# A hybrid decoder layer: gate buffers, load lead times and the minimum of a merge

## The chip, the cores and the metric

The kernel runs on one core of a Trainium2 chip. Its engines are TensorE (PE in the profile, PEld for its weight loads), VectorE (DVE), ScalarE (ACT), GpSimd (POOL) and SyncE (SP), which in this kernel issues the DMA transfers. The metric is the device time of one execution in microseconds.

## The reference

One layer on 2048 tokens of width 1024, in float32, batch 1:

```python
h = rms_norm(x, norm_w)
proj = h @ w_in                                  # 1024 -> all parts below
dn_qkv, dn_z, dn_b, dn_a, swa_q, swa_k, swa_v, swa_z, gates = split(proj)
# branch A: short causal convolution, then the gated delta rule in chunks of 64 (with a triangular solve)
o_dn  = rms_norm(gated_delta_rule(...), dn_norm_w) * silu(dn_z)
y_dn  = o_dn @ w_branch_dn                       # 512 -> 1024
# branch B: three groups of dilated window attention, merged by softmax over their log denominators
alpha = softmax(lses, axis=groups)
o_swa = sum(alpha * outs) * silu(swa_z)
y_swa = o_swa @ w_branch_swa                     # 512 -> 1024
merged = sigmoid(g_dn) * y_dn + sigmoid(g_swa) * y_swa
out = x + merged @ w_out                         # 1024 -> 1024
```

## The kernel before

A matrix product in float32 is made here of three products of rounded parts: each operand is split into a high part (ACT rounds it, L90) and a rest (DVE or POOL subtracts, L91), and TensorE adds high x high, high x rest and rest x high. Names ending in h and l are such pairs.

The program is written as one stream of TensorE work. Every few matmuls it calls `hook`, which counts a tick; `at(delay, fn)` puts other work that many ticks ahead into the stream. A tick in the last stage is half a block (12 matmuls). This fixes the order in which the program is written; the framework's scheduler then makes each engine's own order from it by its model of times and dependences. Through the attention TensorE, ACT, DVE and POOL are pinned to the written order, through the inversion ACT and POOL; in the last stage no engine is, SP neither. Each engine, SP included, then works through its order strictly one by one: an instruction that waits for a semaphore holds all behind it.

The stages: the input projection with the attention of branch B; z and g blocks of the projection (L723 to L725, whose results go to the scratch arrays zscr and gscr; an ACT step at L1158 reads each product), with the triangular inversion, the merge of the three attention groups and the scan of branch A in their background; and the last stage, which the change is mostly about.

*The merge* (`combine`, L1241 to L1279): for each of 16 tiles of 128 tokens it loads the three groups' outputs (oc, two buffers), takes the minimum over the groups on DVE (L1253, written to cs), and goes on with small POOL and ACT steps (`share`, `weigh`, `add`). The next tile's merge is 15 ticks later. DVE meanwhile works at the inversion (Z and M, L1023 to L1026).

*The last stage* (`run`, L1552 on) works on 8 groups of 256 tokens (nb). In each, `fin_y` makes 8 blocks (m) of 128 output columns of both branches: 24 matmuls of 128x256 (L1334 to L1336), the DVE multiply of the product by the gate (L1338, in place in the gate's tile gt4), the POOL sum of both branches (L1340) and the store of the sum to the scratch array mscr (L1341). The gate of a block is loaded from gscr by `g_load` (L1322) into one of four gt4 buffers, written two blocks ahead. A buffer is free again when its block's store has landed. There are 64 blocks, counted 0 to 63.

Beside it run: `o_plan`, which for the next group loads the branches' outputs (od, osw; L1286) and the z gates (two buffers, L1296), and prepares four operands by TensorE transposes (L1303), the DVE product with z (L1304), ACT (L1307) and POOL (L1308); and `wo_chunk`, which takes a quarter of the output weights raw from HBM (L1193), forms sums and splits, and parks two of them (T1 and T4) in scratch (L1202) through one pair of tiles th and tl. `fetch` (L1230) brings the parked ones back in the last group, four transfers of 1 MB.

Last come 8 `group`s of the output projection (L1411) by a seven-product scheme over two by two blocks; `m_load` (L1346) loads a group's merged values from mscr as one tile mt, and `m_op` forms and splits their sums (S1 to S4, L1367 on).

Of the kernel before, what the change touches and what calls it, by code (L numbers as in the profile page):

```python
# [17 lines left out]
H = 4  # L18
# [29 lines left out]
class Net:  # L48
# [1114 lines left out]
    def fin_setup(self, op, fp):  # L1163
        nc, i = self.nc, self.i
        self.fp = fp
        self.dnw = fp.tile([P, 1], F32, name="dnw", bufs=1)
        nc.sync.dma_start(self.dnw, dr(i["dn_norm_w"], 0, [[1, P], [1, 1]]))
        nc.vector.tensor_scalar(out=self.dnw, in0=self.dnw, scalar1=0.25, scalar2=None, op0=ALU.mult)
        self.oh0, self.ol0 = (op.tile([P, KT, 256], F32R, name=n, bufs=1) for n in ("oh", "ol2"))
        self.wbh, self.wbl = (a[:, 0:2].rearrange("p n k c -> p (n k c)").rearrange("p (m k c) -> p m k c", k=KT, c=P)  # L1170
                              for a in (self.hh, self.hl))
        self.W = {n: tuple(a[:, s, 4 * h:4 * h + 4, :] for a in (self.hh, self.hl))
                  for n, (s, h) in (("B11", (2, 0)), ("B21", (2, 1)), ("T3", (3, 0)), ("B22", (3, 1)),
                                    ("T1", (0, 0)), ("T4", (0, 1)))}
# [11 lines left out]
    def wo_chunk(self, c):  # L1186
# [34 lines left out]
        def fifth():  # L1221
            sub(r["B21"], r["B21"], r["T2"])
            put("T2", r["T2"], V)
        for d, fn in ((6, first), (8, second), (10, lambda: park("T1", r["B11"], V)), (12, fourth), (14, fifth),
                      (16, lambda: park("T4", r["B21"], nc.gpsimd))):
            self.at(d, fn)
# [5 lines left out]
    def comb_setup(self, cb):  # L1232
# [3 lines left out]
        self.comb_load(0)  # L1236
        self.at(8, lambda: self.combine(0))

    def comb_load(self, t):
        oc = self.oc = self.cb.tile([P, G, H, 130], F32, name="oc", bufs=2)  # L1240
        self.nc.sync.dma_start(oc.rearrange("p g h c -> p (g h c)"),  # L1241
                               dr(self.oscr, t * P * G * H * 130, [[G * H * 130, P], [1, G * H * 130]]))

    def combine(self, t):
        nc, cb, V = self.nc, self.cb, self.nc.gpsimd
        oc = self.oc
        if t < 15:
            self.comb_load(t + 1)
        sm = cb.tile([P, 4, 12], F32, name="cs", bufs=2)
        nm, ls = oc[:, :, :, 128], oc[:, :, :, 129]  # L1250
        mn, e, c, r = sm[:, 0, 0:4], sm[:, 1, :].rearrange("p (g h) -> p g h", h=H), \
            sm[:, 2, :].rearrange("p (g h) -> p g h", h=H), sm[:, 3, 0:4]
        nc.vector.tensor_reduce(out=mn.unsqueeze(2), in_=nm.rearrange("p g h -> p h g"), axis=mybir.AxisListType.X, op=ALU.min)  # L1253
        V.tensor_tensor(out=e, in0=mn.unsqueeze(1).to_broadcast([P, G, H]), in1=nm, op=ALU.subtract)
# [13 lines left out]
        def add(g):  # L1268
            o = oc[:, 0, :, 0:P]
            V.tensor_tensor(out=o, in0=o, in1=oc[:, g, :, 0:P], op=ALU.add)  # L1270
            if g == 2:
                nc.sync.dma_start(dr(self.osd, t * P * 512, [[512, P], [P, H], [1, P]]), o)
        self.at(1, share)
        for g in range(G):
            self.at(3 + g, lambda g=g: weigh(g))
        for g in (1, 2):
            self.at(4 + g, lambda g=g: add(g))
        if t < 15:
            self.at(15, lambda: self.combine(t + 1))  # L1279

    def o_load(self, t):
        nc, fp = self.nc, self.fp
        self.o = getattr(self, "o", {})
        od, os = (fp.tile([P, H, P], F32, name=n, bufs=2) for n in ("od", "osw"))
        for a, src in ((od, self.odn), (os, self.osd)):
# [8 lines left out]
    def z_load(self, t, b):  # L1294
        z = self.z[t, b] = self.fp.tile([P, H, P], F32, name="z", bufs=2)
        self.nc.sync.dma_start(z, dr(self.zscr, b * 4 * P * T + t * P, [[T, P], [P * T, 4], [1, P]]))  # L1296
# [13 lines left out]
    def o_plan(self, nb, d):  # L1310
        self.z = getattr(self, "z", {})
        for j, (t, b) in enumerate(((2 * nb, 0), (2 * nb, 1), (2 * nb + 1, 0), (2 * nb + 1, 1))):
            self.at(max(1, d + 3 * j - 4), lambda t=t, b=b: self.z_load(t, b))
            self.at(d + 3 * j, lambda t=t, b=b: self.o_prep(t, b))
# [3 lines left out]
    def g_load(self, i):  # L1318
        if i < 64:
            nb, m = divmod(i, 8)  # L1320
            gt = self.gt[i] = self.fp.tile([P, 2, 256], F32, name="gt4", bufs=4)
            self.nc.sync.dma_start(gt, dr(self.gscr, m * P * T + nb * 256, [[T, P], [8 * P * T, 2], [1, 256]]))  # L1322

    def fin_y(self, nb, m):
        nc = self.nc
        self.g_load(8 * nb + m + 2)
        gt = self.gt.pop(8 * nb + m)
# [15 lines left out]
    def m_load(self, g):  # L1343
        if g < 8:
            mt = self.mt[g] = (self.lp if g % 2 == 0 else self.p2).tile([P, KT, 256], F32, name="mt", bufs=1)
            self.nc.sync.dma_start(mt, dr(self.mscr, g * P * 2048, [[2048, P], [256, 8], [1, 256]]))  # L1346

# [8 lines left out]
    def m_op(self, q):  # L1356
# [4 lines left out]
        mt = self.mt[g]  # L1361
        part = {f"A{t + 1}{k + 1}": mt[:, 4 * k:4 * k + 4, t * P:(t + 1) * P] for t in range(2) for k in range(2)}
        name = PROD[i][0]
# [71 lines left out]
    def run(self):  # L1435
# [118 lines left out]
        self.gt, self.mt, self.ss = {}, {}, {}  # L1554
        self.g_load(0)
        self.g_load(1)
        for nb in range(8):
            if nb < 7:
                self.o_plan(nb + 1, 4)
            if nb in (0, 2, 4, 5):  # L1560
                self.wo_chunk((0, 2, 4, 5).index(nb))
            if nb == 6:
                self.at(8, lambda: self.m_load(0))
            for m in range(8):
# [3 lines left out]
                if nb == 7 and m < 4:  # L1568
                    self.at(3, lambda m=m: self.m_op(m))
        self.flush()  # L1570
# [49 lines left out]
```

## Time and profile before

| | us |
|---|---|
| median of 3 runs | 2406.46 (2401.22 to 2412.41) |
| the profiled execution | 2413.96 |
| its span | 2412.2 |
| TensorE busy in the span | 2298.8 |
| last stage, 1990 to 2250: TensorE busy | 218.6 of 260 |

The profiled execution ran at a granted clock of 0.983. A row of the windows gives the stretch, its length, the busy time of PE, PEld, DVE, ACT and POOL with their instructions, the granted clock, the DMA engines' busy share and GB/s. A row of waits reads "engine line <- what ended the wait: total, times, longest". A row of the timeline gives start, length, engine, line, operation and tiles, and in brackets the idle time before it and what ended that. SPq rows are the issuing of transfers, not the transfers themselves. A row of a group gives count, busy time and mean ns of one, then the idle time before it.

### The profile page before, as it was taken

How to read it: one execution, taken by the hardware profiler on the slowest of the kernel's cores; microseconds unless marked ns; L12 is line 12 of the kernel's file. 1: busy time of each engine (PE TensorE's matmuls, PEld its weight loads, DVE VectorE, ACT ScalarE, POOL GpSimd, SP SyncE). 2: the span in 40 equal slices, each digit the busy share in tenths (PEclk: the TensorE clock that was granted, in tenths of full speed). 3: DMA queues.
4: the chain of work that ended last, by engine and by line, in shares of the span. 5: the costliest groups of instructions: out<-in, count | busy, mean ns of one | idle time of the engine just before them, and what ended most of it. 6: DMA issues, size and time to landing. Idle time of an engine off the chain costs nothing. (4 is left out here: it accounts for less than half of the span.)

```text
span 2412.2 us, 43902 instructions
## 1 busy us (share of the span) xinstructions
PE 2298.8 (95%) x15120; PEld 2083.1 (86%) x15120; DVE 1353.8 (56%) x2786; ACT 978.5 (41%) x3151; POOL 1035.3 (43%) x1460
## 2 busy tenths in 40 slices
PE   7999999989999999999999999998999998888899
PEld 7999999889999999787788888886888888888687
DVE  6566576684445545537777759995244115323553
ACT  5345556643434445436666633334333232101121
POOL 6374275564213213206466634446332215433443
PEclk9999999999999999999999999999999999999999
DMA  9989989858887889744444443435767536855742
GB/s 303 322 285 317 276 262 288 258 174 273 249 243 245 259 251 297 207 121 127 129 126 120 110 133 118 134 111 186 201 193 214 168 122 199 226 166 146 240 167 92
DMA packets 556118, 485.82 MB, mean 201 GB/s; under 512 B 68152, under 2 KB 516984, under 8 KB 551928
## 3 DMA queue, kind: packets, MB, share of 16 engines
q1 hardware_dynamic: 555608, 482.95, 65.6%
q8 instruction: 120, 1.97, 0.3%
q14 instruction: 102, 0.84, 0.1%
q10 hardware_dynamic: 288, 0.07, 0.0%
HBM read 280.23 MB, written 202.67 MB: 200 GB/s over the span
## 5 line engine op out<-in xcount | busy, mean ns | idle before, releaser
L723 PE MATMUL mm<-hh,w 128*128 128x512 f32 x1152 | 465.3, 404 | 10.1 <-ACT gt L1158 10.1
L725 PE MATMUL mm<-hh,w 128*128 128x512 f32 x1152 | 459.2, 399 | 0.0
L724 PE MATMUL mm<-hl,w 128*128 128x512 f32 x1152 | 458.8, 398 | 0.0
L436 PE MATMUL mm<-w,hh 128*128 128x256 f32 x1760 | 326.8, 285 | 0.0
L723 PEld LDWEIGHTS mm<-hh,w 128*128 128x128 f32 x1152 | 221.2, 192 | 57.7 <-ACT gt L1158 11.4
L436 PEld LDWEIGHTS mm<-w,hh 128*128 128x128 f32 x1760 | 269.9, 189 | 0.0
L725 PEld LDWEIGHTS mm<-hh,w 128*128 128x128 f32 x1152 | 218.2, 189 | 47.4
L436 PE MATMUL mm<-hh 128*128 128x256 f32 x880 | 256.8, 292 | 0.0
L724 PEld LDWEIGHTS mm<-hl,w 128*128 128x128 f32 x1152 | 218.4, 190 | 42.6
L436 PE MATMUL mm<-hl,hh 128*128 128x256 f32 x880 | 249.0, 283 | 0.3 <-POOL hl L298 0.3
L436 PE MATMUL mm<-hh,hl 128*128 128x256 f32 x880 | 248.9, 283 | 0.0
L436 PE MATMUL mm<-w,hl 128*128 128x256 f32 x880 | 247.6, 281 | 0.0
L91 POOL TENSOR_TENSOR w<-raw,w 128x512 fp32r<-128x512 f32 x68 | 96.9, 1429 | 240.8 <-ACT w L90 223.5
L610 DVE CUSTOM_DVE_ANT_0 p<-sc,mask 128x128 f32<-128x128 f32 (+1 forms) x192 | 70.0, 365 | 216.1 <-PE sc L607 78.5
L371 POOL TENSOR_SCALAR st<-st 128x4 f32<-128x4 f32 x96 | 20.4, 212 | 372.4 <-ACT junk L370 370.4
L436 PEld LDWEIGHTS mm<-hl,hh 128*128 128x128 f32 x880 | 168.6, 192 | 0.8 <-POOL hl L298 0.8
L436 PEld LDWEIGHTS mm<-hh 128*128 128x128 f32 x880 | 168.6, 192 | 0.0
L436 PEld LDWEIGHTS mm<-hh,hl 128*128 128x128 f32 x880 | 168.2, 191 | 0.0
L436 PEld LDWEIGHTS mm<-w,hl 128*128 128x128 f32 x880 | 165.3, 188 | 0.0
L837 DVE SCALAR_TENSOR_TENSOR acc<-xr,cw,acc 128x512 f32<-128x512 f32 x144 | 121.1, 841 | 17.1 <-ACT acc L835 11.5
L594 ACT ACTIVATE kq<-tp 128x256 fp32r<-128x256 f32 x148 | 56.3, 381 | 178.9 <-PE tp L587 177.9
L613 ACT ACTIVATE p<-p,ol 128x128 f32<-128x128 f32 (+1 forms) x192 | 88.1, 459 | 64.0 <-DVE ol L610 63.7
(347 smaller groups left out, 5877.8 us busy)
## 6 DMA issues: line engine op xcount, KB each, us to landing
wdr<-w SPq DMA_DIRECT2D x56, 512.0 KB, 4.7
w<-wdr SPq DMA_DIRECT2D x54, 512.0 KB, 5.2
qk<-qks SPq DMA_DIRECT2D x212, 128.0 KB, 4.3
qks<-rec SPq DMA_DIRECT2D x96, 256.0 KB, 2.8
raw<-in_w_in_dram SPq DMA_DIRECT2D x68, 256.0 KB, 3.5
gscr<-gt SPq DMA_DIRECT2D x64, 256.0 KB, 3.4
gt<-gscr SPq DMA_DIRECT2D x64, 256.0 KB, 4.4
wdr<-hh SPq DMA_DIRECT2D x28, 512.0 KB, 4.6
```

The source lines that it names most:

```text
L91: eng.tensor_tensor(out=l, in0=raw, in1=h.bitcast(F32), op=ALU.subtract)
L371: nc.gpsimd.tensor_scalar(out=st[:, 0:4], in0=st[:, 0:4], scalar1=1.0 / P, scalar2=EPS, op0=ALU.mult, op1=ALU.add)
L436: mm = lambda x, y, **kw: nc.tensor.matmul(o, x, y, skip_group_check=True, **kw)
L594: nc.scalar.activation(h, src, AF.Copy)
L610: nc.vector.tensor_tensor_reduce(out=p[:, lo:hi], in0=sc[:, lo:hi], in1=self.mask[:, slot * P + lo:slot * P + hi], scalar=3e38, scale=-SCA ...
L613: self.at(1, lambda: nc.scalar.activation(p[:, lo:hi], p[:, lo:hi], AF.Exp, bias=ol[:, 128:129], scale=-1.0, accum_out=ol[:, 129:130]))
L723: nc.tensor.matmul(pr, wh[:, k, :], a, start=(k == 0), stop=False)
L724: nc.tensor.matmul(pr, wh[:, k, :], b, start=False, stop=False)
L725: nc.tensor.matmul(pr, wl[:, k, :], a, start=False, stop=(k == KT - 1))
L837: nc.vector.scalar_tensor_tensor(out=acc, in0=xr[:, j:j + 512], scalar=w[:, j:j + 1], in1=acc, op0=ALU.mult, op1=ALU.add)
```

## The change

- Gate tiles gt4: seven buffers instead of four; four loads are written before the first block, and each `fin_y` writes the load four blocks ahead instead of two.
- z tiles: three buffers instead of two, loads written eight ticks ahead of their use instead of four.
- The four `wo_chunk`s are given out from group 0 on at ticks 1, 29, 57 and 85 (in groups 0, 1, 3 and 5) instead of at the starts of groups 0, 2, 4 and 5, and their steps are one to three ticks later behind the raw loads.
- od and osw become halves of one tile "o" in the pool op, two buffers; the same buffers later hold the merged values of the even groups, in two half tiles with a load each. The odd groups use two half tiles in p2. The first merged group's load is written at the start of group 7 instead of eight ticks into group 6, its `m_op`s one tick later.
- The merge's minimum becomes a function of its own (`comb_min`), written six ticks ahead of its `combine`; the first combine is at tick 11 instead of 8, and share, weigh and add are one to two ticks later.

```diff
@@ wo_chunk
-        for d, fn in ((6, first), (8, second), (10, lambda: park("T1", r["B11"], V)), (12, fourth), (14, fifth),
-                      (16, lambda: park("T4", r["B21"], nc.gpsimd))):
+        for d, fn in ((9, first), (10, second), (11, lambda: park("T1", r["B11"], V)), (13, fourth), (15, fifth),
+                      (17, lambda: park("T4", r["B21"], nc.gpsimd))):
@@ comb_setup, comb_min, combine
-        self.at(8, lambda: self.combine(0))
+        self.at(6, self.comb_min)
+        self.at(11, lambda: self.combine(0))
+    def comb_min(self):
+        self.cs = self.cb.tile([P, 4, 12], F32, name="cs", bufs=2)
+        self.nc.vector.tensor_reduce(out=self.cs[:, 0, 0:4].unsqueeze(2), in_=self.oc[:, :, :, 128].rearrange("p g h -> p h g"),
+                                     axis=mybir.AxisListType.X, op=ALU.min)
-        nc.vector.tensor_reduce(out=mn.unsqueeze(2), in_=nm.rearrange("p g h -> p h g"), axis=mybir.AxisListType.X, op=ALU.min)
-        self.at(1, share)
+        self.at(2, share)
-            self.at(3 + g, lambda g=g: weigh(g))
+            self.at(5 + g, lambda g=g: weigh(g))
-            self.at(4 + g, lambda g=g: add(g))
+            self.at(6 + g, lambda g=g: add(g))
+            self.at(9, self.comb_min)
@@ o_load, z_load, o_plan
-        od, os = (fp.tile([P, H, P], F32, name=n, bufs=2) for n in ("od", "osw"))
+        o = self.op.tile([P, 4, 256], F32, name="o", bufs=2).rearrange("p a c -> p (a c)")
+        od, os = (o[:, x * 512:(x + 1) * 512].rearrange("p (h c) -> p h c", c=P) for x in range(2))
-        z = self.z[t, b] = self.fp.tile([P, H, P], F32, name="z", bufs=2)
+        z = self.z[t, b] = self.fp.tile([P, H, P], F32, name="z", bufs=3)
-            self.at(max(1, d + 3 * j - 4), lambda t=t, b=b: self.z_load(t, b))
+            self.at(max(1, d + 3 * j - 8), lambda t=t, b=b: self.z_load(t, b))
@@ g_load, fin_y
-            gt = self.gt[i] = self.fp.tile([P, 2, 256], F32, name="gt4", bufs=4)
+            gt = self.gt[i] = self.fp.tile([P, 2, 256], F32, name="gt4", bufs=7)
-        self.g_load(8 * nb + m + 2)
+        self.g_load(8 * nb + m + 4)
@@ m_load
-            mt = self.mt[g] = (self.lp if g % 2 == 0 else self.p2).tile([P, KT, 256], F32, name="mt", bufs=1)
-            self.nc.sync.dma_start(mt, dr(self.mscr, g * P * 2048, [[2048, P], [256, 8], [1, 256]]))
+            pool, name = (self.p2, "mt") if g % 2 else (self.op, "o")
+            mt = self.mt[g] = [pool.tile([P, 4, 256], F32, name=name, bufs=2) for _ in range(2)]
+            for x, a in enumerate(mt):
+                self.nc.sync.dma_start(a, dr(self.mscr, g * P * 2048 + x * 1024, [[2048, P], [256, 4], [1, 256]]))
@@ run
-        self.g_load(0)
-        self.g_load(1)
+        for j in range(4):
+            self.g_load(j)
-            if nb in (0, 2, 4, 5):
-                self.wo_chunk((0, 2, 4, 5).index(nb))
-            if nb == 6:
-                self.at(8, lambda: self.m_load(0))
+            if nb == 0:
+                for c in range(4):
+                    self.at(1 + 28 * c, lambda c=c: self.wo_chunk(c))
+            if nb == 7:
+                self.m_load(0)
-                    self.at(3, lambda m=m: self.m_op(m))
+                    self.at(4, lambda m=m: self.m_op(m))
```

*SP in the middle of the last stage.* Number behind a tile's name: which tile it is; a gate's tile has one number from its load to its store. Before, a load takes the buffer of the gate four blocks back: gt4_25267 that of gt4_25098, gt4_25299 that of gt4_25144.

```order
L1341 DMA mscr_217<-gt4_25098 128x256
L1322 DMA gt4_25267<-gscr_77 128x2x256
L1341 DMA mscr_217<-gt4_25144 128x256
L1322 DMA gt4_25299<-gscr_77 128x2x256
L1341 DMA mscr_217<-gt4_25178 128x256
L1286 DMA od_25410<-odn_75 128x512
L1341 DMA mscr_217<-gt4_25223 128x256
L1322 DMA gt4_25339<-gscr_77 128x2x256
L1296 DMA z_25366<-zscr_76 128x4x128
L1322 DMA gt4_25375<-gscr_77 128x2x256
L1341 DMA mscr_217<-gt4_25267 128x256
L1286 DMA osw_25411<-osd_216 128x512
```

Now it takes that of the gate seven blocks back: gt4_25285 that of gt4_25024, gt4_25323 that of gt4_25060, gt4_25363 that of gt4_25104, gt4_25404 that of gt4_25148.

```order
L1329 DMA gt4_25249<-gscr_77 128x2x256
L1303 DMA z_25280<-zscr_76 128x4x128
L1348 DMA mscr_217<-gt4_25024 128x256
L1348 DMA mscr_217<-gt4_25060 128x256
L1329 DMA gt4_25285<-gscr_77 128x2x256
L1329 DMA gt4_25323<-gscr_77 128x2x256
L1348 DMA mscr_217<-gt4_25104 128x256
L1329 DMA gt4_25363<-gscr_77 128x2x256
L1348 DMA mscr_217<-gt4_25148 128x256
L1303 DMA z_25338<-zscr_76 128x4x128
L1329 DMA gt4_25404<-gscr_77 128x2x256
L1348 DMA mscr_217<-gt4_25178 128x256
```

Each load still stands one to three rows behind the store of the tile whose buffer it takes; two stores, and then two loads, now sometimes stand together.

*SP at the end of the last stage.* hh_61 and hl_62 are the fetched weights, mt and o_25851 halves or wholes of group 0's merged values, o_26185 a half of group 2's. Before, from gate load 59 to gate load 62 (the load of group 0 as one tile stands far ahead):

```order
L1322 DMA gt4_25894<-gscr_77 128x2x256
L1341 DMA mscr_217<-gt4_25796 128x256
L1230 DMA hh_61<-wpkT10_218 128x2048
L1341 DMA mscr_217<-gt4_25834 128x256
L1230 DMA hl_62<-wpkT11_219 128x2048
L1322 DMA gt4_25926<-gscr_77 128x2x256
L1341 DMA mscr_217<-gt4_25864 128x256
L1322 DMA gt4_25962<-gscr_77 128x2x256
L1341 DMA mscr_217<-gt4_25894 128x256
L1230 DMA hh_61<-wpkT40_220 128x2048
L1230 DMA hl_62<-wpkT41_221 128x2048
L1322 DMA gt4_25996<-gscr_77 128x2x256
```

Now, from the second half of group 0's merged values on; gate load 59 stands two rows ahead, gate loads 60, 61 and 62 are in it, and the next row is gate load 63:

```order
L1355 DMA o_25851<-mscr_217 128x1024
L1329 DMA gt4_25854<-gscr_77 128x2x256
L1348 DMA mscr_217<-gt4_25638 128x256
L1329 DMA gt4_25884<-gscr_77 128x2x256
L1348 DMA mscr_217<-gt4_25676 128x256
L1355 DMA o_26185<-mscr_217 128x1024
L1348 DMA mscr_217<-gt4_25714 128x256
L1329 DMA gt4_25916<-gscr_77 128x2x256
L1231 DMA hh_61<-wpkT10_218 128x2048
L1348 DMA mscr_217<-gt4_25752 128x256
L1231 DMA hl_62<-wpkT11_219 128x2048
L1348 DMA mscr_217<-gt4_25782 128x256
```

Gate loads 60 to 62 stand ahead of the first fetch now, with stores between them, and two half loads of merged values stand among them. On DVE the additions that read group 0's halves now stand between the multiplies of blocks 54 (gt4_25638) and 55 (gt4_25676):

```order
L1345 SCALAR_TENSOR_TENSOR gt4_25638<-gt4_25638,mm_25784 128x512
L91 TENSOR_TENSOR ol2_22980<-o_25850,oh_22979 128x512
L1376 TENSOR_TENSOR raw_25945<-o_25850,o_25851 128x512
L1376 TENSOR_TENSOR raw_25947<-raw_25945,o_25850 128x512
L1345 SCALAR_TENSOR_TENSOR gt4_25676<-gt4_25676,mm_25822 128x512
```

so that the multiply of block 55 comes behind an addition that reads the second half.

*DVE in the inversion.* One piece of the difference, with a minimum of the merge (cs<-oc) among the steps of the inversion:

```order
 L1025 MEMSET M 128x1
 L1023 TENSOR_TENSOR Z<-M 128x3025
-L1253 TENSOR_REDUCE cs<-oc 128x4
 L1024 MEMSET M 128x64
 L1026 TENSOR_REDUCE M<-Z 128x55
 L1025 MEMSET M 128x1
 L1023 TENSOR_TENSOR Z<-M 128x3136
+L1248 TENSOR_REDUCE cs<-oc 128x4
 L1024 MEMSET M 128x64
 L1026 TENSOR_REDUCE M<-Z 128x56
```

The minimum moved behind the next round of the inversion here.

More of the change, by code (lines that the diff above doesn't have):

```diff
@@ L1165, in fin_setup @@
         self.fp = fp
+        self.op = op
         self.dnw = fp.tile([P, 1], F32, name="dnw", bufs=1)
@@ L1242, in comb_load @@
                                dr(self.oscr, t * P * G * H * 130, [[G * H * 130, P], [1, G * H * 130]]))
+    def comb_min(self):
+        self.cs = self.cb.tile([P, 4, 12], F32, name="cs", bufs=2)
+        self.nc.vector.tensor_reduce(out=self.cs[:, 0, 0:4].unsqueeze(2), in_=self.oc[:, :, :, 128].rearrange("p g h -> p h g"),
+                                     axis=mybir.AxisListType.X, op=ALU.min)
     def combine(self, t):
         nc, cb, V = self.nc, self.cb, self.nc.gpsimd
-        oc = self.oc
+        oc, sm = self.oc, self.cs
         if t < 15:
             self.comb_load(t + 1)
-        sm = cb.tile([P, 4, 12], F32, name="cs", bufs=2)
         nm, ls = oc[:, :, :, 128], oc[:, :, :, 129]
@@ L1361, in m_op @@
         mt = self.mt[g]
-        part = {f"A{t + 1}{k + 1}": mt[:, 4 * k:4 * k + 4, t * P:(t + 1) * P] for t in range(2) for k in range(2)}
+        part = {f"A{t + 1}{k + 1}": mt[k][:, :, t * P:(t + 1) * P] for t in range(2) for k in range(2)}
         name = PROD[i][0]
```

## The prediction

> **What bounds the kernel now.** I read the page first, then the last stage by windows, then the waits of SP's queue there, then that queue row by row.
>
> ```profile
> span 2412.2 us, 43902 instructions
> PE 2298.8 (95%) x15120; PEld 2083.1 (86%) x15120; DVE 1353.8 (56%) x2786; ACT 978.5 (41%) x3151; POOL 1035.3 (43%) x1460
> PE mm L1411 6%; DMA mscr<-gt 4%; DMA gt<-gscr 2%; POOL gt L1340 1%; DMA raw<-in_w_out_dram 0%; POOL hl L91 0%; SPq L1322 0%; DVE gt L1338 0%; POOL w L1308 0%; DVE raw L1367 0%; PE mm L1335 0%; PE mm L1336 0%; PE mm L1334 0%; POOL ol L1308 0%; ACT hh L90 0%
> ```
>
> TensorE is 95% busy, so no change here can win much: 113 us are idle in all. The chain that ended last runs back through the output projection (L1411) and then not through TensorE but through two transfers, the store of a merged block (mscr<-gt) and the load of a gate (gt<-gscr). So look at the stage that makes them, from 1990 to 2250 us:
>
> ```profile
> 1990.00:2020.00 30.00, 25.96 (x203) 25.29 (x203) 18.77 (x25) 8.86 (x15) 15.95 (x13) 0.97 0.59 172
> 2020.00:2119.00 99.00, 84.16 (x653) 81.87 (x652) 40.21 (x56) 17.00 (x28) 46.97 (x45) 0.94 0.78 223
> 2119.00:2212.00 93.00, 81.15 (x624) 79.65 (x624) 23.70 (x36) 7.35 (x12) 32.75 (x36) 0.91 0.57 160
> 2212.00:2250.00 38.00, 27.34 (x195) 25.59 (x196) 10.87 (x15) 5.21 (x9) 14.01 (x14) 0.96 0.71 234
> ```
>
> The first number behind the length is TensorE's busy time: 218.6 us of 260, so 41 of the kernel's 113 idle microseconds lie here. What does SP, which issues all the loads and stores, wait for (total, times, longest; first the stretch 2119 to 2212, then the whole stage)?
>
> ```profile
> SPq L1322 <- DMA mscr<-gt: 57.4, 18, 4.2
> SPq L1322 <- DMA mscr<-gt: 103.4, 40, 4.2
> ```
>
> In the steady stretch SP stands for 57.4 of 93 us at the head of its queue, at a gate load, until a store has landed: the load takes the buffer that the store empties. Behind it wait all later loads and stores, of other buffers too. One group of eight blocks in that queue, from one store to the same place a group later:
>
> ```profile
> 2120.01 0.42 SPq L1341 DMA_DIRECT2D mscr<-gt  x1
> ...
> 2124.46 0.37 SPq L1322 DMA_DIRECT2D gt<-gscr  x1
> ...
> 2125.39 0.50 SPq L1341 DMA_DIRECT2D mscr<-gt  x1
> 2129.53 0.36 SPq L1322 DMA_DIRECT2D gt<-gscr  x1
> 2129.99 0.42 SPq L1341 DMA_DIRECT2D mscr<-gt  x1
> 2133.42 0.36 SPq L1322 DMA_DIRECT2D gt<-gscr  x1
> 2133.83 0.46 SPq L1341 DMA_DIRECT2D mscr<-gt  x1
> ...
> 2137.78 0.37 SPq L1322 DMA_DIRECT2D gt<-gscr  x1
> ...
> 2139.27 0.46 SPq L1341 DMA_DIRECT2D mscr<-gt  x1
> ...
> 2143.97 0.37 SPq L1322 DMA_DIRECT2D gt<-gscr  x1
> ...
> 2144.91 0.49 SPq L1341 DMA_DIRECT2D mscr<-gt  x1
> ...
> 2149.71 0.37 SPq L1322 DMA_DIRECT2D gt<-gscr  x1
> ...
> 2151.23 0.42 SPq L1341 DMA_DIRECT2D mscr<-gt  x1
> ```
>
> The period is 2151.23 - 2120.01 = 31.2 us. In it lie six landings one after another, each from the store to the load that needs its buffer: 4.45, 4.14, 3.43, 3.95, 4.70 and 4.80, together 25.5 and 4.24 in the mean; the 5.75 left is issuing. TensorE's own need comes from a stretch where it waits for nothing:
>
> ```profile
> 2227.85 0.28 PE L1334 MATMUL mm<-w,hh 128*128 128x256 f32 x1
> 2230.21 0.28 PE L1336 MATMUL mm<-w,hl 128*128 128x256 f32 x1
> L1303 PE MATMUL tp<-ident,od 128*128 128x128 f32 x24 | 3.6, 272 | 0.0
> ```
>
> The two matmuls are twenty starts apart, 0.118 us each. A group has 8 x 24 matmuls and, by the grouped row for 2119 to 2212 (24 for each of two sources in three groups), 16 transposes: 208 x 0.118 = 24.5 us. The queue's 31.2 is 6.7 longer, so **the queue bounds the stage**.
>
> **The change part by part.** The sum is made against the profiled 2412.2 us; that execution took 2413.96, 7.5 (0.3%) above the median 2406.46.
>
> *Seven gate buffers: a head start.* A load behind a store costs one place in that queue, 31.2 / 8 = 3.9 us a block. Before, four loads have a fresh buffer and wait for no store; after, seven have one. So 57 loads hang on a store instead of 60: 3 x 3.9 = **-11.7 us**, once. That needs the stage's start to have room for them: SP waited there for other things, so it is a gain at best, and its lower end is 0.
>
> *Seven gate buffers: the steady rhythm.* One would expect that a load which is due four blocks later no longer holds anything up. But the order of SP's queue is set by the scheduler, which puts each load nearly where its buffer comes free. Going down the changed queue with one landing wait wherever a load's store has not yet had 4.24 us, I again find six landings in a row per group: two loads that follow each other share one wait, but then a single store stands directly ahead of its load. The issuing between them takes 5.2 instead of 5.75. So 6 x 4.24 + 5.2 = 30.7, **-0.5 us** a group, over some five groups in this state **-2.5**. The bounds are no gain, and TensorE's 24.5 (below, rival B).
>
> *Output weights and z loads earlier.* In the first third of the stage DVE's queue stops at other things:
>
> ```profile
> 2016.80 0.69 DVE L91 TENSOR_TENSOR tl<-raw,th 128x512 fp32r<-128x512 f32 x1 [6.94 <-DMA wpkT<-tl]
> 2029.93 0.69 DVE L1338 SCALAR_TENSOR_TENSOR gt<-gt,mm 128x512 f32<-128x512 f32 x1 [5.76 <-DMA z<-zscr]
> 2057.04 0.69 DVE L1304 SCALAR_TENSOR_TENSOR z<-tp,z 128x512 f32<-128x512 f32 x1 [7.24 <-DMA z<-zscr]
> ```
>
> Two z loads came 5.76 and 7.24 us late: they sat behind landing waits. With a third buffer and four ticks more lead they may come in time, a gain of up to 13.0; but they stand in the same queue, and DVE's next wait is the gate, which comes no sooner. The chunks still use one parking buffer each (th, tl), so the wait of 6.94 for its store stays, and splits of four chunks now lie in groups 0 to 5 at other places. I set this to **0**: the waits overlap the queue's own. Ends: -13.0, and +6.9 for one more such stop.
>
> *The first merged group's load.* It moves from group 6, where the scheduler had put it far forward, into the end of the stage, in two halves. The queue there now:
>
> ```profile
> 2226.90 0.36 SPq L1322 DMA_DIRECT2D gt<-gscr  x1
> ...
> 2228.30 0.47 SPq L1341 DMA_DIRECT2D mscr<-gt  x1
> ...
> 2231.59 0.45 SPq L1341 DMA_DIRECT2D mscr<-gt  x1
> ...
> 2236.22 0.37 SPq L1322 DMA_DIRECT2D gt<-gscr  x1
> ...
> 2239.85 0.37 SPq L1322 DMA_DIRECT2D gt<-gscr  x1
> 2241.43 0.48 SPq L1322 DMA_DIRECT2D gt<-gscr  x1
> 2249.56 0.69 DVE L1338 SCALAR_TENSOR_TENSOR gt<-gt,mm 128x512 f32<-128x512 f32 x1 [0.36 <-DMA gt<-gscr]
> ```
>
> From gate load 59 (2226.90) to the multiply of block 63 (2249.56) it takes 22.7 us. Two of the landings there are long, 2228.30 to 2236.22 = 7.9 and 2231.59 to 2239.85 = 8.3, since the fetches of packed weights (1 MB each) move beside them. In the changed queue the second half of the load (0.5 MB) and a half for group 2 (o_26185, which itself waits until the additions of group 0 have read its buffer) stand between gate loads 59 and 62. Against that two landings are taken out of the row, because loads 60 to 63 empty buffers seven blocks old. Walking the rows with these landings gives 27.6 us: **+5**. Ends: 0 (the extra transfers fly beside existing waits) and +16 (rival C).
>
> *The merge and its minimum.* There are 16 of these DVE reductions at 0.17 us. What they hang on, and what the merge can delay:
>
> ```profile
> 1631.60 0.17 DVE L1253 TENSOR_REDUCE cs<-oc 128x4 f32<-128x12 f32 x1
> 1631.73 4.04 DVE L1023 TENSOR_TENSOR Z<-M 128x3721 f32<-128x3721 f32 x1
> 1657.05 0.18 DVE L1253 TENSOR_REDUCE cs<-oc 128x4 f32<-128x12 f32 x1 [8.76 <-DMA oc<-oscr]
> L723 PE MATMUL mm<-hh,w 128*128 128x512 f32 x1152 | 465.3, 404 | 10.1 <-ACT gt L1158 10.1
> 1600.00:1680.00 80.00, 69.94 (x293) 56.19 (x292) 61.62 (x37) 27.80 (x82) 51.14 (x46) 0.96 0.45 137
> ```
>
> All that TensorE loses by way of ACT in the z and g blocks is 10.1 us, the most to be won; that is also its idle time from 1600 to 1680, where the last merges of the inversion's stage lie. But DVE's order is the scheduler's too, and it had already put the minimum far ahead of its use; in the changed order it falls one round of the matrix inversion later in most places, once behind the 4.04 us row. Two such rows late on POOL, with TensorE following, would be +8.1. I take **0**, between -10.1 and +8.1.
>
> Sum: -11.7 - 2.5 + 0 + 5 + 0 = -9.2. Span 2403, an execution 2405 beside the profiled 2413.96; on the scale of the median 2406.46 - 9.2 = **2397 us**, 0.4% faster.
>
> **The rivals.**
>
> A, the forecast: the queue stays the bound and gives a head start only. The own range is 2386 to 2407: -20 with half of the z gain and no dearer end, and no change when the end costs all that the start wins. Chance 0.50.
>
> B, **the queue lets go.** If a store has mostly landed when its load comes up (the load follows its store by one to three places now, and the buffer is seven blocks old), the stage runs at TensorE's 24.5 us a group. Over the five groups that are at 31.2 this is 5 x 6.7 = 33 us, and with a dearer end 28 or with the z waits up to 45: 2361 to 2380, middle 2373. For it speak 57.4 us of waiting of one kind; against it the order, in which stores still precede their loads closely. Chance 0.20.
> The Trainium skill, "Perfetto Trace Analysis", section Optimization Strategy, says that the same gap returning on the engine that should be saturated can mean too few buffers; by that rule more of them is the cure, and B is what it gives. Another page speaks for B by a price: the Trainium skill, "DMA: Bandwidth & Descriptors", section "Anatomy of one DMA — SWDGE (gpsimd) path", fits a transfer as 2.0 us and its bytes at 436 GB/s, as an estimate from that page 2.3 us for a 128 KB store; six of these and 5.2 would be 19 us a group, and TensorE would bound the stage. The six landings above took 3.43 to 4.80 instead, and by them the queue bounds it.
>
> C, **slower: the end jams.** The load of group 0 in halves joins the four fetches. If the four last landings take the 8.3 us of a landing beside a fetch instead of 4.2, the end grows by 4 x 4.1 = 16; the additions for group 0 stand ahead of the multiply of block 55 in DVE's order and need the second half, whose landing, again 8.3 us, can hold that multiply while the next ones queue behind it. With the head start half eaten by the early chunks (-6), this is 16 + 8 - 6 - 2.5 = +15: 2422. It decides when the second half lands after block 54's multiply. For it: two of four landings are already this long. Against: seven gates are in place by then, so TensorE has a reserve of some blocks. Chance 0.15.
>
> D, **nothing is gained.** Buffers filled ahead of the stage are eaten by the early waits (6.94 on the park stays), the rhythm is the old one: -12 + 7 + 5 = 0, 2406. This is also the case in which the change doesn't load further ahead at all, because the scheduler had the loads at the release of their buffers already. Chance 0.15.
>
> **How the numbers follow.** Below 0.5%, 12 us, this measurement hardly tells a change from none. Under A the sum lies just short of that bound, so its 0.50 goes 0.20 to faster and 0.30 to same; B gives 0.20 to faster; C 0.13 to slower and 0.02 to same; D 0.13 to same and 0.02 to slower. That is faster 0.40, same 0.45, slower 0.15. The range holds A and D and reaches to the middle of B and halfway into C: 2374 to 2417.
>
> **What would show it.** If I am right, SP's waits at the gate load on mscr<-gt stay near 57 us of 93 between the third group and the seventh, and the period of a group near 30.7. The first three groups end some 10 us sooner against the stage's start, and from load 59 to the last multiply it takes more than 22.7. B is shown by a period near 24.5 and SP waiting for POOL's sums (L1347 of the changed kernel) instead of landings. C is shown by landings of 8 us between loads 59 and 63 and a DVE wait for o<-mscr. I am wrong if the inversion's stretch from 1600 to 1680, where TensorE is idle 10 of 80 us, changes by more than 5 us, or if the z waits vanish without the gates becoming late in their place.

## The result and the profile after

The changed kernel takes 2402.43 us in the median of 20 runs (2395.28 to 2406.96), the kernel before 2406.47 in 20 runs beside it. The ratio is 0.9976, with a 95% interval from 0.9966 to 0.9986: 5.8 us faster, with 3.4 to 8.2 as the interval (the ratio is that of the means of all runs; the medians lie 4.0 apart). On a second chip, where the kernel before takes 2412.56, the same kernel measured 0.9965 (0.9952 to 0.9979). The forecast was 9.2 us less, 2397.

The profiled execution of the changed kernel has a span of 2401.8 us, and 2403.63 in all. It is 10.4 us shorter in the span than the profiled one of before, but that one lay 7.5 us above its median; so more than half of the difference between the two traces need not be the change's, and what follows leans on stretches of the stage and on the timed runs beside them.

Three lines of the changed kernel's page (span, engines, chain of waits), and then its windows, with the columns as before:

```profile
span 2401.8 us, 43873 instructions
PE 2289.9 (95%) x15120; PEld 2078.5 (87%) x15120; DVE 1358.6 (57%) x2786; ACT 978.8 (41%) x3151; POOL 1050.3 (44%) x1460
...
PE mm L1420 6%; DMA mscr<-gt 2%; PE mm L1341 1%; PE mm L1342 1%; PE mm L1343 1%; DMA gt<-gscr 1%; DMA mt<-mscr 0%; POOL gt L1347 0%; DVE gt L1345 0%; DVE raw L1376 0%; DMA o<-mscr 0%; DMA raw<-in_w_out_dram 0%; PE tp L1310 0%; SPq L1329 0%; POOL ol L1315 0%
```

```profile
2020.00:2119.00 99.00, 88.77 (x702) 87.67 (x703) 44.94 (x59) 17.83 (x29) 49.89 (x50) 0.92 0.74 207
2119.00:2212.00 93.00, 77.38 (x596) 75.80 (x595) 22.39 (x33) 7.58 (x12) 30.40 (x33) 0.93 0.60 170
2212.00:2250.00 38.00, 30.43 (x192) 27.94 (x193) 14.69 (x21) 7.43 (x12) 13.39 (x14) 0.87 0.80 280
```

From 2020 to 2119 TensorE works 4.6 us more than before, from 2119 to 2212 3.8 us less. The chain at the end still runs through the store and the load, now with matmuls of the blocks between (L1341 to L1343). SP's waits from 2119 to 2212 are what they were (57.4 us before), and the timeline of its queue shows a group of eight blocks:

```profile
SPq L1329 <- DMA mscr<-gt: 57.9, 19, 4.5
```

```profile
2119.15 0.42 SPq L1348 DMA_DIRECT2D mscr<-gt  x1
...
2123.91 0.37 SPq L1329 DMA_DIRECT2D gt<-gscr  x1
...
2124.89 0.92 SPq L1348 DMA_DIRECT2D mscr<-gt  x2
2129.23 0.88 SPq L1329 DMA_DIRECT2D gt<-gscr  x2
2130.21 0.42 SPq L1348 DMA_DIRECT2D mscr<-gt  x1
2134.19 0.36 SPq L1329 DMA_DIRECT2D gt<-gscr  x1
...
2138.21 0.36 SPq L1329 DMA_DIRECT2D gt<-gscr  x1
...
2142.72 0.37 SPq L1329 DMA_DIRECT2D gt<-gscr  x1
...
2147.71 0.37 SPq L1329 DMA_DIRECT2D gt<-gscr  x1
...
2149.23 0.42 SPq L1348 DMA_DIRECT2D mscr<-gt  x1
```

Six stops again, with pairs of stores and of loads (x2) that share one, and a period of 30.1 us here; over two groups, from the store of block 32 (2130.21) to that of block 48 (2191.51, read from the same view), it is 30.65 a group. Before, the same two groups took 31.74 each.

What changed is the reserve. The table is put together from the starts of DVE's multiplies (L1338 before, L1345 after) and of the stores in the timelines, counted from the multiply of block 0:

| block | multiply before, us | multiply after, us | store behind its multiply, before, us | the same, after, us |
|---|---|---|---|---|
| 16 | 71.3 | 70.8 | 1.5 | 2.1 |
| 32 | 126.9 | 117.0 | 9.6 | 17.2 |
| 48 | 190.2 | 178.3 | 9.8 | 17.2 |
| 54 | 214.8 | 205.4 | 7.7 | 14.2 |
| 55 | 218.5 | 222.4 | 7.7 | 3.6 |
| 63 | 252.2 | 242.4 | 1.5 | 1.5 |

With three more gates TensorE and DVE run some 7.5 us further ahead of the store queue, and twelve ahead of their old times at block 48. The store of block 48 is only 4.5 us sooner, counted in the same way (195.5 beside 200.0). Between blocks 54 and 55 that reserve is spent at once, in DVE's timeline on the wait for the second half of group 0's merged values (idle time and what ended it in brackets; the first multiply shown is that of block 55, the last two are those of blocks 62 and 63):

```profile
2206.36 0.69 DVE L91 TENSOR_TENSOR ol<-o,oh 128x512 fp32r<-128x512 f32 x1 [4.28 <-ACT oh L90]
2217.05 0.69 DVE L1376 TENSOR_TENSOR raw<-o 128x512 f32<-128x512 f32 x1 [9.99 <-DMA o<-mscr]
2217.77 0.69 DVE L1376 TENSOR_TENSOR raw<-raw,o 128x512 f32<-128x512 f32 x1
2218.38 0.68 DVE L1345 SCALAR_TENSOR_TENSOR gt<-gt,mm 128x512 f32<-128x512 f32 x1
...
2235.50 0.69 DVE L1345 SCALAR_TENSOR_TENSOR gt<-gt,mm 128x512 f32<-128x512 f32 x1 [2.15 <-PE mm L1343]
2238.40 0.69 DVE L1345 SCALAR_TENSOR_TENSOR gt<-gt,mm 128x512 f32<-128x512 f32 x1 [2.21 <-PE mm L1343]
```

TensorE stands behind that multiply for 8.40 us, as its own timeline has it:

```profile
2219.12 0.58 PE L1341 MATMUL mm<-w,hh 128*128 128x256 f32 x1 [8.40 <-DVE gt L1345]
```

Behind the hold the gates lie ready, and the eight blocks to the last one take 20.0 us. Their last multiplies wait for TensorE's matmuls and not for a gate, 2.84 to 2.90 us apart.

### The profile page after: what moved, and what is told of

The parts are those of the page before. It is cut to its first block, busy times and chain, and to the rows that moved or that the text cites. A ratio compares the mean times of both kernels' runs of the same rounds, so it can differ in the third digit from the quotient of the medians.

```text
span 2401.8 us, 43873 instructions
## 1 busy us (share of the span) xinstructions
PE 2289.9 (95%) x15120; PEld 2078.5 (87%) x15120; DVE 1358.6 (57%) x2786; ACT 978.8 (41%) x3151; POOL 1050.3 (44%) x1460
## 5 line engine op out<-in xcount | busy, mean ns | idle before, releaser
L91 POOL TENSOR_TENSOR w<-raw,w 128x512 fp32r<-128x512 f32 x68 | 103.3, 1522 | 224.0 <-ACT w L90 216.3
L837 DVE SCALAR_TENSOR_TENSOR acc<-xr,cw,acc 128x512 f32<-128x512 f32 x144 | 120.9, 840 | 17.3 <-ACT acc L835 11.8
```

The source lines that it names most:

```text
L91: eng.tensor_tensor(out=l, in0=raw, in1=h.bitcast(F32), op=ALU.subtract)
L837: nc.vector.scalar_tensor_tensor(out=acc, in0=xr[:, j:j + 512], scalar=w[:, j:j + 1], in1=acc, op0=ALU.mult, op1=ALU.add)
```

## The experiments

Each run states its ratio to the kernel before on the chip that it ran on; the kernel before took 2412.44, 2412.56 and 2409.11 us in the three sets. A difference between two kernels of a set is taken from their medians, each of 4 to 12 runs.

### Is it SP's queue?

The first set takes the stores out of SP's queue, in the changed kernel and in the kernel before, and then the two half loads of group 0's merged values.

The first edit, in `fin_y`, of the changed kernel (e1) and of the kernel before (e2):

```diff
-        nc.sync.dma_start(dr(self.mscr, nb * P * 2048 + m * 256, [[2048, P], [1, 256]]), gt[:, 0, :])
+        nc.scalar.dma_start(dr(self.mscr, nb * P * 2048 + m * 256, [[2048, P], [1, 256]]), gt[:, 0, :])
```

> The changed kernel with one edit: the stores of the merged blocks (mscr<-gt) are issued by ACT, not by SP; the gate loads stay on SP. Theory (SP's in-order queue with six landings in a row per group bounds the last stage): SP's waits at the gate load on mscr<-gt fall from 57.9 us of the 93 between 2119 and 2212 to under 10, the period of eight blocks falls from 30.7 us to 24.5 to 26, and the whole falls from 2402 to 2375 to 2388. Rival (the stage is bound by what TensorE's operands wait for, or by a landing that a load needs in any case): the waits only change their place and the time stays within 5 us of 2402.

Measured: 2373.61 us, ratio 0.9846 (0.9823 to 0.9868). The same kernel in a later set gave 2379.17, 0.9867 (0.9845 to 0.9889). That is some 30 us below the changed kernel by the ratios, a little more than the queue theory had (2375 to 2388). Its window from 2119 to 2212 has TensorE busy 91.29 of 93 us, where it was 77.38, and the waits of SP in that window hold a surprise:

```profile
2119.00:2212.00 93.00, 91.29 (x750) 89.54 (x750) 34.97 (x48) 11.87 (x19) 41.48 (x44) 1.00 0.73 231
```

```profile
SPq L1329 <- DMA mscr<-gt: 46.0, 23, 4.9
```

I had expected under 10 us of waits. SP still stops 46.0 us at landings, since the scheduler still puts each load where its buffer comes free; but no store stands behind the loads any more. From the multiply of block 32 to that of 48 it takes 48.6 us, 24.3 a group, beside the 24.5 worked out for TensorE. The stores don't land faster for coming from ACT: from issue to landing they took 4.2 us in the median of this window, and 3.9 in the changed kernel. The granted clock is 1.00 in the window, where it was 0.93; as an estimate, a group of 24.3 would take 26.1 at 0.93, so the clock accounts for at most 1.8 of the 6.4 us that a group gains. So a wait at the head of a queue costs what stands behind it, and not its own length.

> The kernel before with the same single edit: stores by ACT, four gate buffers. Theory (the queue, not the number of buffers): a buffer's own loop is a landing of 4.2, a load of 4.4, multiply and sum 1.5 and two issues of 0.4, about 11 us for four blocks, which is just TensorE's 4 x 2.83 = 11.3; so already the kernel before gains most of what the same edit gains on the changed one: 2380 to 2393. Rival (too few buffers): it stays at 2400 or above, and only with seven buffers does the edit pay.

Measured: 2385.4 us, ratio 0.9895 (0.9874 to 0.9917). Four buffers are enough for the rhythm once the queue is free: blocks 32 to 48 took 48.2 us, and in the same window TensorE works nearly without a gap, though SP stood 59.0 us of it at landings. (The profiled execution took 2397.1 us, 11.7 above the median; only its rhythm is read here.)

```profile
2119.00:2212.00 93.00, 92.02 (x783) 91.62 (x782) 33.15 (x47) 11.17 (x18) 44.52 (x48) 1.00 0.70 202
```

By ratio, 0.9895 against 0.9976, the kernel before with stores by ACT is some 19 us faster than the changed kernel with its stores on SP (17 against the 0.9965 of the second chip; measured on different chips, so to some microseconds only). The number of buffers was not what bounded the stage.

The first merged group's load, in `m_load` of the changed kernel (e3; e4 has e1's edit too):

```diff
-                self.nc.sync.dma_start(a, dr(self.mscr, g * P * 2048 + x * 1024, [[2048, P], [256, 4], [1, 256]]))
+                (self.nc.sync if g else self.nc.scalar).dma_start(a, dr(self.mscr, g * P * 2048 + x * 1024, [[2048, P], [256, 4], [1, 256]]))
```

> The changed kernel with one edit: the two half loads of the first merged group are issued by ACT, so they don't stand behind landing waits in SP's queue. Theory: DVE's wait of 9.99 us for o<-mscr ahead of block 55's multiply, and TensorE's 8.4 us behind it, go down to under 3; as the gate loads of the end still come at the queue's pace, 4 to 8 us of it are won: 2394 to 2399. Rival (the end goes at the pace of the gate loads in any case, the hold only takes up slack): within 2 us of 2402.

Measured: 2409.35 us, ratio 0.9986 (0.9972 to 0.9999), which is 2403.1 on the scale of 2406.47: not faster than the changed kernel. The wait did go, and the time didn't follow; DVE's timeline in this run:

```profile
2209.74 0.69 DVE L1376 TENSOR_TENSOR raw<-o 128x512 f32<-128x512 f32 x1 [1.91 <-DMA o<-mscr]
...
2221.91 0.69 DVE L1345 SCALAR_TENSOR_TENSOR gt<-gt,mm 128x512 f32<-128x512 f32 x1 [2.15 <-PE mm L1343]
...
2232.37 0.69 DVE L1345 SCALAR_TENSOR_TENSOR gt<-gt,mm 128x512 f32<-128x512 f32 x1 [6.44 <-DMA gt<-gscr]
2238.76 0.69 DVE L1345 SCALAR_TENSOR_TENSOR gt<-gt,mm 128x512 f32<-128x512 f32 x1 [5.70 <-DMA hh<-wpkT]
```

DVE waits 1.91 for the half load instead of 9.99, and the multiply of block 60 comes at 2221.91, 7.9 us sooner than in the changed kernel. But the last gates don't: load 63 is issued at 2228.14 here and at 2228.55 there, and lands, beside the fetches, at 2238.57 here and at 2237.51 there. So blocks 62 and 63 wait 6.44 and 5.70 (the last row names a fetch that was under way, but the gate landed 0.19 us before the multiply), and the last multiply is at 2238.76 beside 2238.40. The rival's account holds: without the hold the end goes at the pace of the gate loads on SP. In the changed kernel it goes at TensorE's pace behind the hold, and counted from block 0 the two last multiplies lie 1.1 us apart (243.5 and 242.4), so taking away the hold alone wins nothing.

> Both edits of the changed kernel together. Theory: with the stores gone from SP's queue the half loads are no longer late there, so the second edit adds little to the first: within 5 us of the run with the stores alone, 2373 to 2388. Rival (two causes that add): 4 to 8 us below the run with the stores alone.

Measured: 2374.84 us, ratio 0.9845 (0.9825 to 0.9865), 1.2 us from the stores alone. The second edit adds nothing to the first.

### Which part of the change pays?

The second set holds the changed kernel itself and three partial undoings.

> The changed kernel once more, unedited, as the common reference for the three runs beside it on the same chip. Theory: 0.2 to 0.3% below the kernel before, as measured (ratio 0.9976).

Measured: 2404.29 us, ratio 0.9965 (0.9952 to 0.9979), a little lower than the first time; the two intervals overlap.

e6 is the changed kernel with four gates:

```diff
-            gt = self.gt[i] = self.fp.tile([P, 2, 256], F32, name="gt4", bufs=7)
+            gt = self.gt[i] = self.fp.tile([P, 2, 256], F32, name="gt4", bufs=4)
-        self.g_load(8 * nb + m + 4)
+        self.g_load(8 * nb + m + 2)
-        for j in range(4):
+        for j in range(2):
             self.g_load(j)
```

> The changed kernel with the gate buffers undone: four gt4 tiles, two loads ahead of the stage, each block's load written two blocks ahead; all else as changed. Theory (the win is the head start of three loads, nothing in the rhythm): the period of eight blocks stays 31 us, DVE's multiplies in groups 4 to 6 come some 10 us later against the stage's start, and the time is 4 to 10 us above the changed kernel, so at the kernel before or just over it. Rival (the gates bring nothing, z and weights do): within 2 us of the changed kernel.

Measured: 2414.07 us, ratio 1.0005 (0.9994 to 1.0016), 9.8 us above the changed kernel beside it and at the time of the kernel before: without the gates the other parts together gain nothing. From block 0's multiply to that of block 32 it takes 129.3 us against 119.3 in the changed kernel of this set, and to block 63 252.6 against 243.5. In between the lead is gone once: at block 55 both stand at the half load and go on at 223.0 and 223.6. With seven gates the eight blocks behind it then take 20.0 us, with four 29.6. The period of the stores from block 32 to 48 was 29.7 a group here (I had said 31), and 31.4 in the changed kernel: the rhythm of the two doesn't differ beyond its own scatter. What seven gates win is won once, three places in the queue, some 10 us.

e7 is the changed kernel with the z loads and the weight chunks undone (the steps of a chunk, too, are at their old ticks):

```diff
-        z = self.z[t, b] = self.fp.tile([P, H, P], F32, name="z", bufs=3)
+        z = self.z[t, b] = self.fp.tile([P, H, P], F32, name="z", bufs=2)
-            self.at(max(1, d + 3 * j - 8), lambda t=t, b=b: self.z_load(t, b))
+            self.at(max(1, d + 3 * j - 4), lambda t=t, b=b: self.z_load(t, b))
...
-            if nb == 0:
-                for c in range(4):
-                    self.at(1 + 28 * c, lambda c=c: self.wo_chunk(c))
+            if nb in (0, 2, 4, 5):
+                self.wo_chunk((0, 2, 4, 5).index(nb))
```

> The changed kernel with z and the output weights undone: two z tiles loaded four ticks ahead, the four weight chunks given out and stepped as before; seven gates stay. Theory (these edits are worth nothing, their waits overlap the queue's): within 3 us of the changed kernel, with DVE's z waits of 5 to 7 us back in groups 1 to 3. Rival (up to 13 us of z waits were won): 5 to 13 us above the changed kernel.

Measured: 2404.77 us, ratio 0.9965 (0.995 to 0.998), 0.5 us from the changed kernel: these edits are worth nothing here. Block 32 comes later without them (123.8 us after block 0, against 119.3), but block 63 doesn't (239.2 against 243.5). Their waits had not come back in full either: from 1995 to 2090 DVE waits for z 7.7 us in three parts, the longest 4.7. Of the changed kernel, the stretch from 1990 to 2068, DVE's waits:

```profile
DVE raw L1206 <- DMA raw<-in_w_out_dram: 16.8, 4, 12.1
DVE gt L1345 <- PE mm L1343: 9.9, 3, 6.4
DVE tl L91 <- DMA wpkT<-tl: 9.6, 1, 9.6
DVE hl L91 <- ACT hh L90: 4.2, 1, 4.2
```

The same stretch of the kernel before:

```profile
DVE hl L91 <- ACT hh L90: 12.2, 2, 7.0
DVE raw L1205 <- DMA raw<-in_w_out_dram: 7.8, 5, 2.4
DVE z L1304 <- DMA z<-zscr: 7.2, 1, 7.2
DVE tl L91 <- DMA wpkT<-tl: 6.9, 1, 6.9
DVE gt L1338 <- DMA z<-zscr: 5.8, 1, 5.8
DVE gt L1338 <- DMA gt<-gscr: 2.9, 1, 2.9
```

The 13.0 us of z waits are gone, and so are 8.0 of the waits for ACT and 2.9 for a gate. In their place there are 9.0 more for the raw weights, 2.7 more for the park and 9.9 for TensorE's products. In all DVE waits 40.5 us instead of 42.8, and block 16 comes after 70.8 us instead of 71.3. The waits changed their names.

e8 is the changed kernel with the merge undone; `combine` calls `comb_min` itself, at the old place of the reduction:

```diff
-        self.at(6, self.comb_min)
-        self.at(11, lambda: self.combine(0))
+        self.at(8, lambda: self.combine(0))
...
+        self.comb_min(oc)
-        self.at(2, share)
+        self.at(1, share)
-            self.at(5 + g, lambda g=g: weigh(g))
+            self.at(3 + g, lambda g=g: weigh(g))
-            self.at(6 + g, lambda g=g: add(g))
+            self.at(4 + g, lambda g=g: add(g))
-            self.at(9, self.comb_min)
```

> The changed kernel with the merge undone: the minimum inside combine again, combine, share, weigh and add at their old ticks. Theory (the scheduler had the minimum ahead anyway): within 2 us of the changed kernel, TensorE busy 70 of 80 us from 1600 to 1680. Rival (the merge's spacing matters for ACT): 3 to 8 us above or below, seen in TensorE's wait for ACT at L1158 (7.6 us in the changed kernel).

Measured: 2406.61 us, ratio 0.9977 (0.9965 to 0.9989), 2.3 us above the changed kernel, between the two accounts; the intervals overlap, so the time alone doesn't tell. TensorE is busy 70.16 of the 80 us from 1600 to 1680, as expected. Its wait for ACT over all the z and g blocks moves with the edit, though. The group's row on the page, first of the changed kernel, then of the run with the merge undone:

```profile
L723 PE MATMUL mm<-hh,w 128*128 128x512 f32 x1152 | 463.5, 402 | 7.6 <-ACT gt L1158 7.6
```

```profile
L723 PE MATMUL mm<-hh,w 128*128 128x512 f32 x1152 | 465.2, 404 | 10.0 <-ACT gt L1158 10.0
```

It is 9.2 to 10.1 us in the three profiles with the old merge (the kernel before, e2 and e8), and 7.2 to 8.0 in the ten with the new one: 2.4 us between the changed kernel and e8 that agree with the 2.3. ACT's waits from 1600 to 1700 (total, times, longest) changed their places, first in the kernel before, then in the changed one:

```profile
ACT oc L1266 <- POOL cs L1262: 21.7, 5, 8.2
ACT cs L1257 <- POOL cs L1254: 14.9, 3, 7.6
```

```profile
ACT cs L1262 <- POOL cs L1259: 25.2, 3, 11.1
ACT oc L1271 <- POOL cs L1267: 14.2, 5, 5.3
```

The weighing waits 14.2 instead of 21.7, the exponential (L1262) 25.2 instead of 14.9, so in the two together ACT waits 2.8 us more than before. Why TensorE waits less for it was not shown, and the later weighing and the earlier minimum were not separated.

### What do the parts do once the queue is free?

> The changed kernel with its stores issued by ACT once more, as the reference for the two runs beside it. Theory: ratio 0.985 to the kernel before, as measured.

Measured: 2379.17 us, ratio 0.9867 (0.9845 to 0.9889).

> Stores by ACT, with the gate buffers undone (four, two ahead), z and weights as changed. The kernel before with stores by ACT was some 12 us slower than the changed one with it, all of it lost in the first 16 blocks (80.4 us against 69.4 from the first multiply to that of block 16). Theory (without the queue four buffers suffice, and the lost time is that of z loads and weight chunks): within 4 us of the run beside it with seven gates, 70 to 73 us for the first 16 blocks. Rival (the head start of three gates is what is missing there): 8 to 13 us slower than that run, near 80 us for the first 16 blocks.

Measured: 2379.84 us, ratio 0.9878 (0.9858 to 0.9899): 0.7 us from the run beside it. With the stores off SP the three extra gates gain nothing that can be measured in the time, to some microseconds. The first 16 blocks took 72.6 us. The profile, of an execution 4.8 us above the median, does show four gates short at the end: from block 54 to block 63 it takes 37.3 us against 26.4 in the run beside it, and from 2190 to 2226 DVE waits 15.5 us for gates, beside the fetches. Part of that comes back behind block 63, from where the span ends after 159.5 us instead of 163.6.

> Stores by ACT with seven gates, and z and weights undone. Theory (cover gone): the z and weight edits, worth nothing beside the full queue, are worth 8 to 12 us here, so this run is that much slower than the one with both, near 80 us for the first 16 blocks. Rival (the gates do it): within 4 us, 69 to 73 us for the first 16 blocks.

Measured: 2376.49 us, ratio 0.9848 (0.9821 to 0.9875), the first 16 blocks 70.3 us. My theory falls: z and weights are worth nothing here either. Neither part alone explains the 80.4 us that stand in e2's profile. But that profile is of an execution 11.7 us above e2's median, at a granted clock of 0.88 from 2020 to 2119 where e1's had 0.93, and it is 26.0 us longer than e1's, while the medians lie 11.8 apart. So the 80.4 need not be usual. What makes up the 11.8 stays open: the kernel before lacks both parts, has the old merge, and has another place for the first merged group's load.

## Why the prediction was right or wrong

**The bound.** Right. "SP's waits stay near 57 us of 93" was 57.9, the period "near 30.7" was 30.65 in the one profile and 31.4 in the other (over the same two groups the kernel before had 31.74; the prediction's 31.2 was one group), and e1 and e2 show the queue directly: without the stores in it a group takes 24.1 to 24.3 us, TensorE's own time as worked out from two matmul rows.

**The head start, -11.7, and the rhythm, -0.5 a group.** Right in kind, and slightly too large. Undoing the gates costs 9.8 us (e6), to be set beside -11.7 - 2.5 + 5, which is what the prediction gave to gates and end together, -9.2. The trace bears out the place in the queue: counted from block 0's multiply, gate load 59 is issued after 215.2 us instead of 229.6, 14.3 sooner where 11.7 + 2.5 were worked out, and with four gates (e6) after 229.1. The rhythm's half microsecond is smaller than the scatter of the period, 29.7 to 31.4 among three profiles. The sign named for it came late: at block 24, where the third group is over, only 5.9 us were won, and the 10 came by block 32.

**The end, +5.** Right in size, but by luck. From load 59 (2211.23) to the multiply of block 63 (2238.40) it took 27.2 us, where 27.6 was worked out and 22.7 stood before. The 27.6 was a walk along landings; in the trace SP waited only 8.2 us for landings in this stretch, 2.9 at the longest, and the last multiplies waited for TensorE. What filled the 27.2 was DVE's hold, up to 2218.38, and then eight blocks in 20.0 us. The half loads in the queue are not enough to explain it either: with them and four gates (e6) the stretch took 23.4. DVE's hold for the second half, which the prediction gave to rival C, did happen, and longer than C had it: 9.99 us, not 8. C's price failed because the hold fell on the reserve: counted from block 0, the multiplies were 13.9 us ahead of their old times by block 52, and e3 shows that without the hold the last gate comes no sooner. One sign of C, a slow landing, was there for the last gate: load 63 took 9.0 us.

**z loads and weights, 0.** Right by e7. But the reason was half right only: the z waits did vanish, which I had named as a sign against me if the gates didn't become late in their place. What came late instead were the raw weights, the park and TensorE's products.

**The merge, 0.** Probably mis-sized: about -2.4 us by TensorE's wait at L1158, with e8's 2.3 beside it, which is within the noise. It lies inside the bounds of -10.1 to +8.1. I had looked only at the minimum's place in DVE's order, and left out that weigh now comes three ticks behind share instead of two; whether that is the reason was not shown. The stretch from 1600 to 1680 gave no sign against the prediction: TensorE was busy 70.77 us of 80 after and 69.94 before.

**The sum.** The forecast of -9.2 lies just outside the interval of the first measurement (-3.4 to -8.2) and inside that of the second, whose ratio gives -8.4. Gates, merge and the rest as measured, -9.8 - 2.3 + 0, give -12; the changed kernel is 5.8 and 8.4 us below the kernel before. What takes some 4 to 6 back is not among the parts undone here: the first merged group's place and the joint tile o were not undone alone. This stays open, and may be within the error of the differences, each of some 3 us.

**The rivals.** B, the queue letting go, didn't come by this change. Its price was about right: its middle was 2373, and e1, where the queue does let go, gives 0.9846 of 2406.47, 2369, in one set and 0.9867, 2374, in the other. (The top of its range, 28 us less, works out as 2378 and not 2380.) C came in its first step, the hold, and not in its end. D falls with e6.

Two rules spoke for B. The Trainium skill, "Perfetto Trace Analysis", section Optimization Strategy, takes gaps that return for a possible sign of too few buffers; here three more buffers took the period of the gap from 31.74 to 30.65 us only. The Trainium skill, "DMA: Bandwidth & Descriptors", section "Anatomy of one DMA — SWDGE (gpsimd) path", has a fit for transfers of the gpsimd path that gives 2.3 us for 128 KB as an estimate; the landings that SP waited for here, of stores issued by SP, took 3.43 to 4.80.

## What to carry to other kernels

When loads and stores share one in-order queue, a load that waits for a store's landing stops everything behind it. As long as each load stands close behind the store that frees its buffer, as the scheduler put it here, more buffers change only how many loads have no such store: the win is one place in the queue per buffer, once. Look at the order of the queue, not at the distance between load and use. Issuing the stores from an engine with time to spare took the kernel before to 0.9895, three to four times what the change wins (0.9965 to 0.9976), and the changed kernel to 0.985 to 0.987.

## What the runs showed of the hardware

A queue's waits alone say little of its price: SP waited 57.9 us of 93 for landings in the changed kernel, 46.0 in e1 and 59.0 in e2, and the stretch held 596 of TensorE's matmuls in the first, 750 in the second and 783 in the third. In e1 the issue of the stores cost ACT no time that TensorE waited long for: from 1995 to 2250 TensorE waited 0.8 us for ACT, and 14.3 us in the kernel before.
